# FFN of a two-layer encoder trunk: two tiles kept on chip as one down chunk in 8 PSUM banks, the last wo weights loaded ahead of the FFN's first, DRAM operands split in program order, operands at 512-byte starts

## The chip, the cores and the metric

The kernel runs on one core of a Trainium2 chip. The metric is device time in microseconds (us) of one launch on that core, as the median of several runs. One further run was profiled, and its trace is what the rows below come from. The engines are TensorE (PE; its weight loads are PEld), VectorE (DVE), ScalarE (ACT), GpSimd (POOL) and SyncE (SP), which issues most of the DMAs. PE's clock has two levels, 1.2 and 2.4 GHz; the profile gives the granted clock of a stretch as a share of the higher one.

## What is computed

An encoder of two layers over 1024 tokens of width 1024: a mixer with a residual, then a gated feed-forward network (FFN) with a residual, then a final norm. The change touches the FFN, the end of each mixer and the addresses of the operands.

```python
def reference(x, ...):
    h = x
    for layer in range(2):
        hn = rmsnorm(h, attn_norm_g[layer])
        if layer % 2 == 0:
            mix = hybrid_pool_mla(hn, ...)   # pooling and latent attention, then @ w_out
        else:
            mix = diff_block(hn, ...)        # differential attention, then @ w_out
        h = h + mix
        h = h + swiglu(rmsnorm(h, ffn_norm_g[layer]), ffn_w_gate[layer], ffn_w_up[layer], ffn_w_down[layer])
    return rmsnorm(h, final_norm_g)

def swiglu(h, w_gate, w_up, w_down):          # hidden width 2816 = 22 tiles of 128
    return (jax.nn.silu(h @ w_gate) * (h @ w_up)) @ w_down
```

## The kernel before

Everything is held transposed: 8 row tiles `o` of 128 features by 1024 tokens, the tokens in two halves `hf` of 512. Each fp32 product is made of three matmuls on operands split into a high and a low part (`mm3`, L160 to L164): high by high (L162), high by low (L163), low by high (L164). ACT makes the high part by a cast, DVE (in places POOL) the low part by a subtraction, so each weight tile needs a DMA into a raw tile, a cast and a subtraction before PE can use it. The raw tiles of the `weights` pool have 3 slots, the split ones 4 (`whi`, `wlo`).

**End of a mixer (`residual`, L674 on).** The mixer's output projection runs over the row tiles in the order of `PAIRS` (0, 4, 1, 5, 2, 6, 3, 7). DVE adds each result to the residual (L683; the tiles are `hT` in layer 0, `hB` in layer 1), and ACT and DVE make the FFN's operands from it: `b11`, `t2` and others, high and low parts of sums and differences of quarters of the activations. The weights of the projection are `wob0` to `wob7` in layer 0 (named `raw_wob`, `whi_wob`, `wlo_wob`) and `wdb0` to `wdb7` in layer 1. For the last pair, 3 and 7, half 0 of both is computed before half 1 of both; half 1 of a tile is written after DVE has added its half 0. In the loop the FFN's first weights (`load_first`: `raw_a11`, `raw_a21`, `raw_a22`, and their sums `s1` to `s3` on POOL, L776) are loaded at `i == 3`.

**Gate and up (`gate_up`).** For each of 22 tiles `ff` of the hidden width, 7 products (`PRODUCTS`, a Strassen scheme on the 2 by 2 quarters) of 4 mm3 each, so 84 matmuls, go into 4 banks. `prep` splits a weight tile for a product (L794, L795); every fifth pair lies in `s_pool` (names `wh`, `wl`), the others in the `weights` pool (`whi`, `wlo`). `after` turns the banks into an activation tile `u` of 128 by 1024; tiles 0 to 19 go to DRAM (`asp`), 20 and 21 stay.

**Down.** `CHUNKS` sets the order: (20), (21), then five chunks of 4 tiles. A step is one chunk and one row tile `o`: for each half, a bank takes 3 matmuls for each tile of the chunk, and DVE adds the bank to `hd` (L948), which `down_begin` has fetched from DRAM on POOL's queue. There are 8 banks. A step's weights (`raw_d`, L928; `whi_d`, `wlo_d`) are 128 columns wide for each tile. From chunk (21) on, the operands of the next chunks are fetched (`araw`), cast (`ah`, L916) and subtracted (`al`, L917) by `slot`.

What stands on an engine runs in the order of a list scheduler, which works on the program's order and its own estimates; `tc.keep_in_program_order` and `tc.high_priority` steer it.

Of the kernel before, what the change touches and what calls it, by code (L numbers as in the profile page):

```python
# [43 lines left out]
def encoder_trunk(ctx: ExitStack, tc: tile.TileContext, A: dict):  # L44
# [9 lines left out]

    def pad(p, name):

        p.tile([P, 8], F32, name=name, tag="pad", bufs=1)

    pad(spool, "pad_s")
    pad(rpool, "pad_r")  # L60

# [50 lines left out]
    dve.memset(onec, 1.0)  # L112
    pad(cpool, "pad_c")
    ones_f = cpool.tile([P, P], F32, name="ones_f")
# [562 lines left out]
    def residual(norm, spill, load, run, ffn):  # L677
# [9 lines left out]
        for i, o in enumerate(PAIRS[:6]):  # L687
            for j in (i, i + 1, i + 2):
                load(PAIRS[j])
            ps = run(o, (0, 1))  # L690
            for hf in range(2):
                norm.square(o, hf, out(o, hf, ps[hf]))
            if i % 2:
                norm.firsts(i // 2, hT)
                if i > 2:
                    norm.rest(i // 2 - 1, hT, (1,))
            elif i:
                norm.rest(i // 2 - 1, hT, (0,))
            if i == 3:
                ffn.load_first()  # L700
# [38 lines left out]
    class FeedForward:  # L739
# [67 lines left out]
        def after(self, ff, i):  # L807
# [34 lines left out]
        def gate_up(self, ps):  # L842
# [38 lines left out]
            for k, (ff, i) in enumerate(work):  # L881
# [9 lines left out]
                if k == len(work) - 2:  # L891
                    self.next_weights(0)
                    self.next_weights(1)
                self.product(ff, i)
                if k < len(work) - 1:
                    self.after(ff, i)
                if (ff, i) == (NFF - 2, 6):
                    self.keep_halves(ff)

        def keep_halves(self, ff):  # L900
            u = self.keep[ff]["u"]
            hi, lo = ([self.g_pool.tile([P, HT], F32R, tag="raw", name=f"a{w}{i}_{self.L}_{ff}", bufs=6)
                       for i in range(2)] for w in "hl")
            for i in range(2):
                act.copy(hi[i], u[:, half(i)])
                dve.tensor_tensor(lo[i], u[:, half(i)], f(hi[i]), ALU.subtract)
            self.seen[ff] = [(hi[i], lo[i]) for i in range(2)]


        seen = property(lambda self: self.__dict__.setdefault("_seen", {}))  # L910

        def slot(self, ff, src):
# [3 lines left out]
            act.copy(hi, src)  # L916
            dve.tensor_tensor(lo, src, f(hi), ALU.subtract)  # L917
            self.seen[ff] = [(hi[:, half(i)], lo[:, half(i)]) for i in range(2)]

        def operand(self, ff):  # L920
            raw = self.a_pool.tile([P, T], F32, tag="araw", name=f"araw{self.L}_{ff}", bufs=2)
            nc.sync.dma_start(raw, asp[ff])
            self.slot(ff, raw)

# [26 lines left out]
        def down_begin(self, a_pool, hpool, n_slots):  # L951
# [6 lines left out]
            self.after(NFF - 1, 6)  # L958
            self.slot(NFF - 1, self.keep[NFF - 1]["u"])
            self.held = 1  # L960
            self.ahead = [ff for c in self.CHUNKS[2:] for ff in c]
            self.down_steps(range(8), None, None)

        def down_steps(self, ks, finish, between_halves):
            last = len(self.CHUNKS) - 1
            for k in ks:
                c, o = self.steps[k]
                self.next_weights(k + 2)

# [7 lines left out]
                if o == 7 and c:  # L977
                    self.held -= len(self.CHUNKS[c])
# [624 lines left out]
```

## Time and profile before

| | us |
|---|---|
| median of 3 runs | 2656.02 (2654.16 to 2659.57) |
| profiled run | 2657.84 |
| span of its trace | 2656.1 |
| PE busy | 2538.1 (96%) |
| DVE busy | 1705.3 (64%) |
| ACT busy | 1065.4 (40%) |

PE is busy in all but 118 us of the span, so what matters is where those lie and how long a matmul takes. A row of the timeline shows when an instruction started, how long it took, and in brackets how long its engine had stood before it and what released it. A matmul's own duration overlaps the next; the step from one start to the next is its price.

### The profile page before, as it was taken

Reading aid. Unit: us, or ns where it says so; the run is one execution under the profiler, and the core shown is the slowest. Engines: PE = TensorE matmul, PEld = TensorE weight load, DVE = VectorE, ACT = ScalarE, POOL = GpSimd, SP = SyncE. Lnnn points to the kernel's source line nnn. Section 1 sums busy time; section 2 is a strip of 40 time slices with the busy share of each in tenths; the row PEclk is TensorE's granted clock in tenths of the full one; section 3 lists DMA queues with packets and bytes.
Section 4 is the critical chain, followed back from the end, with each engine's and each line's share of the span. In section 5 each row is a group of like instructions: output and inputs, shape, how many; then the busy total and the mean of one; then the engine's idle time right before and its main releaser. Section 6 shows DMA issues by size and latency. Waiting matters only on the chain. (4 is left out here: it accounts for less than half of the span.)

```text
span 2656.1 us, 31575 instructions
## 1 busy us (share of the span) xinstructions
PE 2538.1 (96%) x11334; PEld 1993.0 (75%) x11334; DVE 1705.3 (64%) x2932; ACT 1065.4 (40%) x1888; POOL 759.5 (29%) x582
## 2 busy tenths in 40 slices
PE   8999999899999989999999999999989999989997
PEld 6777887688888868886666666666768888877886
DVE  7467776866666664455677677676586566656444
ACT  4236666533333321243555555544353333332222
POOL 4224443422222100033434343333342222210002
PEclk9999999999999999999999999999999999999998
DMA  3010001622222152322111111114452222233321
GB/s 132 32 44 15 17 9 42 171 79 92 75 92 72 56 179 80 111 99 63 33 40 44 36 48 33 36 44 159 131 134 86 81 78 89 76 122 113 111 76 64
DMA packets 129580, 205.50 MB, mean 77 GB/s; under 512 B 11664, under 2 KB 56720, under 8 KB 129424
## 3 DMA queue, kind: packets, MB, share of 16 engines
q1 hardware_dynamic: 123088, 187.76, 21.3%
q0 software_dynamic: 6336, 15.73, 2.4%
q8 instruction: 89, 1.46, 0.2%
q14 instruction: 67, 0.55, 0.1%
HBM read 145.25 MB, written 46.66 MB: 72 GB/s over the span
## 5 line engine op out<-in xcount | busy, mean ns | idle before, releaser
L162 PE MATMUL d<-ah,whi_d 128*128 128x512 f32 x640 | 254.4, 398 | 22.5 <-DVE hd L948 17.0
L948 DVE TENSOR_TENSOR hd<-hd,d 128x512 f32<-128x512 f32 x224 | 150.4, 684 | 184.8 <-PE d L164 184.7
L163 PE MATMUL d<-al,whi_d 128*128 128x512 f32 x640 | 254.3, 397 | 0.0
L164 PE MATMUL d<-ah,wlo_d 128*128 128x512 f32 x640 | 248.1, 393 | 0.4 <-DVE wlo_d L933 0.3
L509 ACT CAST pth<-pt 128x512 fp32r<-128x512 f32 x256 | 145.6, 586 | 159.4 <-PE pt L506 156.2
L776 POOL TENSOR_TENSOR s<-s,raw_a 128x512 f32<-128x512 f32 x88 | 117.0, 1330 | 319.5 <-DVE wlo_s L795 231.0
L510 DVE TENSOR_TENSOR ptl<-pt,pth 128x512 fp32r<-128x512 f32 x256 | 169.9, 686 | 54.6 <-ACT pth L509 53.0
L1226 DVE CUSTOM_DVE_ANT_0 e<-s,nd 128x512 f32<-128x512 f32 x256 | 169.1, 686 | 42.6 <-PE s L1224 39.7
L776 POOL TENSOR_TENSOR s<-raw_a,raw_a 128x512 f32<-128x512 f32 x88 | 117.7, 1337 | 262.4 <-DVE wlo_s L795 207.0
L794 ACT CAST whi_s<-s 128x512 fp32r<-128x512 f32 x142 | 88.1, 621 | 242.9 <-PE p L163 232.8
L1239 ACT ACTIVATE e<-e,nm 128x1024 f32<-128x1024 f32 x128 | 146.4, 1147 | 68.5 <-DVE nm L1234 68.4
L506 PE MATMUL pt<-ident,e 128*128 128x128 f32 x1024 | 156.6, 281 | 9.1 <-POOL e L500 4.6
L162 PEld LDWEIGHTS d<-ah,whi_d 128*128 128x128 f32 x640 | 121.5, 190 | 56.0 <-issue 17.2
L506 PEld LDWEIGHTS pt<-ident,e 128*128 128x128 f32 x1024 | 125.5, 144 | 48.2 <-DVE ptl L510 11.2
L932 ACT CAST whi_d<-raw_d 128x512 fp32r<-128x512 f32 (+1 forms) x104 | 53.9, 521 | 260.4 <-PE d L163 208.7
L164 PEld LDWEIGHTS d<-ah,wlo_d 128*128 128x128 f32 x640 | 121.3, 190 | 27.9 <-DVE wlo_d L933 1.9
L163 PEld LDWEIGHTS d<-al,whi_d 128*128 128x128 f32 x640 | 121.7, 190 | 25.5 <-DVE al L917 0.8
L1248 POOL TENSOR_SCALAR e<-e,c 128x1024 f32<-128x1024 f32 x48 | 57.3, 1193 | 276.7 <-DVE c L1244 99.9
L794 ACT CAST whi_a<-raw_a 128x512 fp32r<-128x512 f32 x106 | 65.7, 621 | 138.2 <-PE p L163 137.6
L1221 PE MATMUL s<-KS,QS 128*128 128x512 f32 x256 | 97.2, 428 | 24.4 <-DVE mx L1226 23.3
L1249 POOL TENSOR_TENSOR e<-e,e 128x1024 f32<-128x1024 f32 x48 | 117.1, 2439 | 3.4
L795 DVE TENSOR_TENSOR wlo_s<-s,whi_s 128x512 fp32r<-128x512 f32 x142 | 115.4, 813 | 0.1
(492 smaller groups left out, 6861.6 us busy)
## 6 DMA issues: line engine op xcount, KB each, us to landing
raw_a<-in_w_gate_dram SPq DMA_DIRECT2D x88, 256.0 KB, 2.9
raw_a<-in_w_up_dram SPq DMA_DIRECT2D x88, 256.0 KB, 2.6
asp<-u SPq DMA_DIRECT2D x40, 512.0 KB, 2.9
araw<-asp SPq DMA_DIRECT2D x40, 512.0 KB, 3.7
raw_d<-in_w_down_dram SPq DMA_DIRECT2D x80, 256.0 KB, 2.8
hd<-hs POOLq DMA_DIRECT2D x16, 512.0 KB, 8.5
acc_f<-sq_f POOLq DMA_DIRECT2D x28, 256.0 KB, 4.3
hT<-in_xT_dram SPq DMA_DIRECT2D x16, 256.0 KB, 5.4
```

The lines of the kernel that those rows point to most:

```text
L162: pe.matmul(ps, sh, mh, start=start, stop=False, skip_group_check=onto)
L163: pe.matmul(ps, sh, ml, start=False, stop=False, skip_group_check=onto)
L164: pe.matmul(ps, sl, mh, start=False, stop=stop, skip_group_check=onto)
L506: pe.transpose(pt[:, blk(j)], es[j][:, blk(kt)], ident)
L509: act.copy(hi, pt)
L510: dve.tensor_tensor(lo, pt, f(hi), ALU.subtract)
L776: pool.tensor_tensor(t, r[ff, a], r[ff, b], op)
L794: act.copy(hi, self.raws[ff, n])
L948: dve.tensor_tensor(s, s, b, ALU.add)
L1226: dve.tensor_tensor_reduce(out=e[m][:, half(hf)], in0=ps[m], in1=nd[:, k0 + hf * HT : k0 + hf * HT + HT], scale=1.0, scalar=-3.0e38, op0=A ...
L1239: act.activation(e[m], e[m], AF.Exp, bias=nm, scale=slope, accum_out=l)
L1249: pool.tensor_tensor(e0, e0, e1, ALU.add)
```

## The change

Five parts. The pads that shift the pools are resized (`pad_s` is dropped, `pad_r` is 480 bytes, `pad_c` is 64, and `gsub` moves to the constants), which puts the start of the `weights` pool at byte 18432 of a partition instead of 18368, that is at 0 instead of 448 within 512, and with it the tiles of `temps`, `gate_up` and several other pools. Of some 9,940 matmuls with 512 columns, 7,440 had a stationary operand that started 448 bytes into a 512-byte line, and 2,044 such a moving operand; now none has. In `residual` the weights of the projection are loaded one step earlier and the FFN's first ones one step later. Chunks (20) and (21) become one, (20, 21), whose weights come as 4 loads of 512 columns (`first_weights`) and whose 16 results are evicted once instead of twice. Tile 21's half 0 is finished and split one product earlier. Preps of tile 1, and the splits of the DRAM operands, are held in program order.

```diff
-    pad(spool, "pad_s")
-    pad(rpool, "pad_r")
+    pad(rpool, "pad_r", 480)
...
-    pad(cpool, "pad_c")
+    pad(cpool, "pad_c", 64)
...
-            for j in (i, i + 1, i + 2):
+            for j in range(i, min(i + 4, 8)):
                 load(PAIRS[j])
...
-            if i == 3:
+            if i == 4:
                 ffn.load_first()
...
-        CHUNKS = ((20,), (21,), (0, 1, 2, 3), (4, 5, 6, 7), (8, 9, 10, 11), (12, 13, 14, 15), (16, 17, 18, 19))
+        CHUNKS = ((20, 21), (0, 1, 2, 3), (4, 5, 6, 7), (8, 9, 10, 11), (12, 13, 14, 15), (16, 17, 18, 19))
...
+            pin = tc.keep_in_program_order if ff == 1 else lambda x: x
...
-            act.copy(hi, self.raws[ff, n])
-            dve.tensor_tensor(lo, self.raws[ff, n], f(hi), ALU.subtract)
+            pin(act.copy(hi, self.raws[ff, n]))
+            pin(dve.tensor_tensor(lo, self.raws[ff, n], f(hi), ALU.subtract))
...
                 if i == 0:
-                    self.after(ff, i)
+                    with tc.high_priority(offset=150):
+                        self.after(ff, i)
...
+                if (ff, i) == (NFF - 1, 5):
+                    self.finish_half(ff, 0)
+                    self.keep_half(ff, 0, "c", 4)
...
+        def keep_half(self, ff, hf, tag, bufs):
+            u = self.keep[ff]["u"][:, half(hf)]
+            hi, lo = (self.g_pool.tile([P, HT], F32R, tag=tag, name=f"a{w}{hf}_{self.L}_{ff}", bufs=bufs)
+                      for w in "hl")
+            act.copy(hi, u)
+            dve.tensor_tensor(lo, u, f(hi), ALU.subtract)
+            self.seen.setdefault(ff, {})[hf] = hi, lo
...
+        def first_weights(self, q):
+
+            L, ffs = self.L, self.CHUNKS[0]
+            raw = wpool.tile([P, HT], F32, tag="raw", name=f"raw_d{L}_f{q}", bufs=3)
+            nc.sync.dma_start(
+                raw.rearrange("p (a b) -> p a b", a=2),
+                A["w_down"][L][ffs[0] : ffs[-1] + 1, :, 2 * q * P : (2 * q + 2) * P].rearrange("a p b -> p a b"))
...
-            self.slot(NFF - 1, self.keep[NFF - 1]["u"])
-            self.held = 1
-            self.ahead = [ff for c in self.CHUNKS[2:] for ff in c]
-            self.down_steps(range(8), None, None)
+            self.keep_half(NFF - 1, 1, "c", 4)
+            self.held = 0
+            self.ahead = [ff for c in self.CHUNKS[1:] for ff in c]
+            for g in range(2):
+                os = range(4 * g, 4 * g + 4)
+                if g:
+                    self.next_operands()
+                    self.first_weights(2)
+                    self.first_weights(3)
+                banks = {}
+                for j, ff in enumerate(self.CHUNKS[0]):
+                    for hf in range(2):
+                        for o in os:
+                            if j == 0:
+                                banks[o, hf] = self.bank(f"d{L}_f_{o}_{hf}")
+                            mm3(banks[o, hf], *self.ws["first", o // 2].block(2 * j + o % 2), *self.seen[ff][hf],
+                                j == 0, j == 1)
+                            if j:
+                                s = self.h[o][:, half(hf)]
+                                dve.tensor_tensor(s, s, banks[o, hf], ALU.add)
```

On DVE in layer 1, from the finish of the last activation tile `u1_21` to the second row tile's additions, there stood before:

```order
L838 TENSOR_TENSOR u1_21_20424<-u1_21_20424,rb_f1_17159 128x1024
L917 TENSOR_TENSOR al1_0_20714<-araw1_0_20711,ah1_0_20713 128x1024
L917 TENSOR_TENSOR al1_1_20720<-araw1_1_20717,ah1_1_20719 128x1024
L917 TENSOR_TENSOR al1_21_20569<-u1_21_20424,ah1_21_20568 128x1024
L933 TENSOR_TENSOR wlo_d1_0_6_20637<-raw_d1_0_6_20638,whi_d1_0_6_20636 128x128
L948 TENSOR_TENSOR hd1_0_20547<-hd1_0_20547,d1_0_0_0_20578 128x512
L948 TENSOR_TENSOR hd1_0_20547<-hd1_0_20547,d1_0_0_1_20583 128x512
```

The same place now, where `d1_f_0_0` is the bank of row tile 0, half 0, of the joint chunk:

```order
L919 TENSOR_TENSOR u1_21_20325<-u1_21_20325,rb_f1_17060 128x512
L913 TENSOR_TENSOR al1_1_21_20476<-u1_21_20325,ah1_1_21_20475 128x512
L1000 TENSOR_TENSOR hd1_0_20454<-hd1_0_20454,d1_f_0_0_20479 128x512
L1000 TENSOR_TENSOR hd1_0_20454<-hd1_0_20454,d1_f_0_1_20495 128x512
L1000 TENSOR_TENSOR hd1_1_20455<-hd1_1_20455,d1_f_1_0_20483 128x512
L1000 TENSOR_TENSOR hd1_1_20455<-hd1_1_20455,d1_f_1_1_20499 128x512
L955 TENSOR_TENSOR wlo_d1_1_0_20668<-raw_d1_1_0_20669,whi_d1_1_0_20667 128x512
L1000 TENSOR_TENSOR hd1_2_20456<-hd1_2_20456,d1_f_2_0_20487 128x512
```

The splits of the DRAM operands (`al1_0`, `al1_1`) stood ahead of the first addition and stand behind the eighth now, outside this piece.

On SP near the end of layer 0's mixer, the difference in the order of the loads (`hs0` is the residual's copy to DRAM):

```order
+L134 DMA raw_wob3_0_0_4672<-in_wo_b_dram 128x512
 L684 DMA hs0_4499<-hT0_93 128x512 x2
-L768 DMA raw_a21_0_0_4721<-in_w_up_dram 128x512
+L134 DMA raw_wob7_0_0_4727<-in_wo_b_dram 128x512
 L684 DMA hs0_4499<-hT4_97 128x512 x2
+L768 DMA raw_a11_0_0_4774<-in_w_gate_dram 128x512
 L684 DMA hs0_4499<-hT1_94 128x512 x2
-L768 DMA raw_a22_0_0_4723<-in_w_up_dram 128x512
+L768 DMA raw_a21_0_0_4776<-in_w_up_dram 128x512
 L684 DMA hs0_4499<-hT5_98 128x512 x2
-L134 DMA raw_wob3_0_0_4733<-in_wo_b_dram 128x512
```

The last two weights of the projection moved ahead of the three first weights of the FFN; in layer 1 `raw_wdb3` and `raw_wdb7` moved in the same way.

On ACT in layer 1's residual, the cast of `whi_wdb3` stood here before, behind the scaling of the second pair:

```order
L649 ACTIVATE sq_f1_1_0_16874<-hB1_15705 128x512
L640 ACTIVATE b11h1_f1_16725<-hB1_15705,cols_88 128x512
L649 ACTIVATE sq_f1_1_1_16879<-hB1_15705 128x512
L664 ACTIVATE x_f1_0_16882<-hB0_15704,cols_88 128x512
L135 CAST whi_wdb3_0_16957<-raw_wdb3_0_0_16959 128x512
L637 CAST t1h0_f1_16743<-t1_f1_0_16883 128x512
L637 CAST t2h0_f1_16731<-t2_f1_0_16884 128x512
L637 CAST t3h0_f1_16737<-x_f1_0_16882 128x512
L135 CAST whi_wdb7_0_17006<-raw_wdb7_0_0_17008 128x512
```

And now:

```order
L135 CAST whi_wdb3_0_16797<-raw_wdb3_0_0_16799 128x512
L649 ACTIVATE sq_f1_1_0_16781<-hB1_15606 128x512
L640 ACTIVATE b11h1_f1_16626<-hB1_15606,cols_87 128x512
L649 ACTIVATE sq_f1_1_1_16786<-hB1_15606 128x512
L664 ACTIVATE x_f1_0_16789<-hB0_15605,cols_87 128x512
L637 CAST t1h0_f1_16644<-t1_f1_0_16790 128x512
L637 CAST t2h0_f1_16632<-t2_f1_0_16791 128x512
L135 CAST whi_wdb7_0_16852<-raw_wdb7_0_0_16854 128x512
```

The cast of `whi_wdb3` moved ahead by four places and that of `whi_wdb7` by one, and the loads of both stand ahead of the FFN's on SP, as in layer 0.

## Rows read from the trace of the kernel before

**Rows 1.** The page, part 1: busy us, share of the span, instructions.
```profile
PE 2538.1 (96%) x11334; PEld 1993.0 (75%) x11334; DVE 1705.3 (64%) x2932; ACT 1065.4 (40%) x1888; POOL 759.5 (29%) x582
```
**Rows 2.** Stretches: us; busy us (xinstructions) of each engine; clock, DMA share, GB/s.
```profile
515.00:540.00 25.00, 20.52 (x88) 16.03 (x88) 17.33 (x30) 10.29 (x18) 12.41 (x11) 0.86 0.36 82
...
937.90:974.50 36.60, 27.08 (x98) 19.08 (x96) 29.95 (x51) 10.93 (x21) 0.00 (x0) 0.86 0.57 197
974.50:1195.00 220.50, 220.50 (x962) 180.42 (x963) 110.46 (x155) 60.06 (x88) 21.09 (x16) 1.00 0.32 102
...
2376.80:2416.70 39.90, 26.50 (x98) 19.63 (x96) 33.89 (x56) 14.05 (x25) 1.92 (x4) 0.87 0.67 241
```
**Rows 3.** Waits of PE: line waited for, total us, times, longest us.
```profile
PE d L162 <- DVE hd L948: 17.0, 6, 7.6
PE od L162 <- DVE hB L683: 7.6, 1, 7.6
...
PE d L162 <- ACT whi_d L932: 5.5, 4, 1.9
PE ob L162 <- DVE hT L683: 4.8, 1, 4.8
...
PE p L162 <- DVE u L824: 3.9, 2, 3.3
```
**Rows 4.** Timeline of PE, start of down in layer 1: start, us, instruction, wait.
```profile
2382.05 0.39 PE L164 MATMUL d<-ah,wlo_d 128*128 128x512 f32 x1
2390.02 0.77 PE L162 MATMUL d<-ah,whi_d 128*128 128x512 f32 x1 [7.58 <-DVE hd L948]
2390.59 0.63 PE L163 MATMUL d<-al,whi_d 128*128 128x512 f32 x1
```
**Rows 5.** Timeline of DVE, the same place.
```profile
2387.86 1.22 DVE L917 TENSOR_TENSOR al<-u,ah 128x1024 fp32r<-128x1024 f32 x1
...
2389.20 1.28 DVE L948 TENSOR_TENSOR hd<-hd,d 128x512 f32<-128x512 f32 x2
```
**Rows 6.** Groups by line and form on DVE, layer 1's down: busy us, mean ns.
```profile
L948 DVE TENSOR_TENSOR hd<-hd,d 128x512 f32<-128x512 f32 x112 | 75.0, 683 | 93.4 <-PE d L164 93.3
L917 DVE TENSOR_TENSOR al<-araw,ah 128x1024 fp32r<-128x1024 f32 x20 | 24.4, 1222 | 12.1 <-ACT ah L916 11.9
```
**Rows 7.** DMA issues between 2370 and 2420: count, KB each, us to landing.
```profile
hd<-hs POOLq DMA_DIRECT2D x8, 512.0 KB, 9.1
```
**Rows 8.** Timeline of PE, three products of tile 21, layer 1, first matmuls.
```profile
2360.37 0.39 PE L162 MATMUL p<-t2h_f,whi_s 128*128 128x512 f32 x1
...
2363.12 0.39 PE L162 MATMUL p<-t3h_f,wh_s 128*128 128x512 f32 x1
...
2365.84 0.39 PE L162 MATMUL p<-t1h_f,whi_s 128*128 128x512 f32 x1
```
**Rows 9.** Timeline of PE, layer 1's last chunk, 48 matmuls apart.
```profile
2592.56 0.39 PE L162 MATMUL d<-ah,lwh 128*128 128x512 f32 x1
...
2603.44 0.39 PE L162 MATMUL d<-ah,lwh 128*128 128x512 f32 x1
```
**Rows 10.** Timeline of PE, layer 1's residual, the last pair of row tiles.
```profile
1940.78 0.80 PE L162 MATMUL od<-yh,whi_wdb 128*128 128x512 f32 x1 [7.59 <-DVE hB L683]
```
**Rows 11.** Timeline of ACT, layer 1's residual.
```profile
1918.62 0.62 ACT L135 CAST whi_wdb<-raw_wdb 128x512 fp32r<-128x512 f32 x1 [4.55 <-DMA raw_wdb<-in_w_do_dram]
...
1924.58 0.62 ACT L135 CAST whi_wdb<-raw_wdb 128x512 fp32r<-128x512 f32 x1 [3.78 <-DMA raw_wdb<-in_w_do_dram]
```
**Rows 12.** Timeline of DVE, the same residual.
```profile
1919.80 1.37 DVE L638 TENSOR_TENSOR t1l_f<-t_f,t1h_f 128x512 fp32r<-128x512 f32 x1 [2.23 <-ACT t1h_f L637]
...
1926.38 0.75 DVE L641 SCALAR_TENSOR_TENSOR b21l_f<-hB,cols,b21h_f 128x512 fp32r<-128x512 f32 x1 [2.15 <-ACT b21h_f L640]
```
**Rows 13.** Timeline of DVE, layer 0: in the residual, and at the start of gate and up.
```profile
485.45 0.69 DVE L136 TENSOR_TENSOR wlo_wob<-raw_wob,whi_wob 128x512 fp32r<-128x512 f32 x1 [1.91 <-ACT whi_wob L135]
...
524.70 0.69 DVE L795 TENSOR_TENSOR wl_s<-s,wh_s 128x512 fp32r<-128x512 f32 x1 [3.08 <-ACT wh_s L794]
```

More of the change, by code (lines that the diff above doesn't have):

```diff
@@ L53, in encoder_trunk, with pad @@
     rpool = tc.alloc_tile_pool(name="edge", bufs=1, side="right")
-    def pad(p, name):
-        p.tile([P, 8], F32, name=name, tag="pad", bufs=1)
-    pad(spool, "pad_s")
-    pad(rpool, "pad_r")
+    def pad(p, name, n):
+        p.tile([P, n // 4], F32, name=name, tag="pad", bufs=1)
+    pad(rpool, "pad_r", 480)
     def new_pool(name, side, bufs=1):
@@ L121, in encoder_trunk @@
     nc.sync.dma_start(cols, A["cols"])
+    gsub = cpool.tile([P, 1], F32, name="gsub")
     def col(i):
@@ L897, in gate_up, with finish_half, operand @@
                 if (ff, i) == (NFF - 2, 6):
[L898 to L907, printed above, removed]
+                    for hf in range(2):
+                        self.keep_half(ff, hf, "raw", 6)
+                if (ff, i) == (NFF - 1, 5):
[8 more added lines that the diff above has]
+            self.seen.setdefault(ff, {})[hf] = hi, lo
+        def finish_half(self, ff, hf):
+            g, u = (self.keep[ff][k][:, half(hf)] for k in "gu")
+            dve.tensor_tensor(u, u, g, ALU.mult)
+            dve.tensor_tensor(u, u, self.norm.rb[:, half(hf)], ALU.mult)
         seen = property(lambda self: self.__dict__.setdefault("_seen", {}))
-        def slot(self, ff, src):
+        def operand(self, ff):
+            raw = self.a_pool.tile([P, T], F32, tag="araw", name=f"araw{self.L}_{ff}", bufs=2)
+            nc.sync.dma_start(raw, asp[ff])
             hi = self.a_pool.tile([P, T], F32R, tag=f"s{self.n_seen % self.n_slots}h", name=f"ah{self.L}_{ff}")
@@ L915, in slot @@
             self.n_seen += 1
-            act.copy(hi, src)
-            dve.tensor_tensor(lo, src, f(hi), ALU.subtract)
+            tc.keep_in_program_order(act.copy(hi, raw))
+            tc.keep_in_program_order(dve.tensor_tensor(lo, raw, f(hi), ALU.subtract))
             self.seen[ff] = [(hi[:, half(i)], lo[:, half(i)]) for i in range(2)]
[L920 to L923, printed above, removed]
+        def first_weights(self, q):
[4 more added lines that the diff above has]
+                A["w_down"][L][ffs[0] : ffs[-1] + 1, :, 2 * q * P : (2 * q + 2) * P].rearrange("a p b -> p a b"))
+            hi, lo = w_pair(f"d{L}_f{q}")
+            act.copy(hi, raw)
+            dve.tensor_tensor(lo, raw, f(hi), ALU.subtract)
+            self.ws["first", q] = W([(hi, lo)])
         def weights(self, c, o, pair):
@@ L958, in down_begin, with next_operands @@
             self.after(NFF - 1, 6)
-            self.slot(NFF - 1, self.keep[NFF - 1]["u"])
-            self.held = 1
-            self.ahead = [ff for c in self.CHUNKS[2:] for ff in c]
-            self.down_steps(range(8), None, None)
+            self.keep_half(NFF - 1, 1, "c", 4)
[9 more added lines that the diff above has]
+                for j, ff in enumerate(self.CHUNKS[0]):
+                    for hf in range(2):
+                        for o in os:
[6 more added lines that the diff above has]
+                                dve.tensor_tensor(s, s, banks[o, hf], ALU.add)
+            self.next_weights(8)
+            self.next_weights(9)
+        def next_operands(self):
+            while self.ahead and self.held < self.n_slots:
+                self.operand(self.ahead.pop(0))
+                self.held += 1
         def down_steps(self, ks, finish, between_halves):
@@ L968, in down_steps @@
                 self.next_weights(k + 2)
-                while c and self.ahead and self.held < self.n_slots:
-                    self.operand(self.ahead.pop(0))
-                    self.held += 1
+                self.next_operands()
                 for hf in range(2):
@@ L976, in down_steps @@
                         finish(o, hf, s)
-                if o == 7 and c:
+                if o == 7:
                     self.held -= len(self.CHUNKS[c])
```

7 lines of the change are left out of this document (4 added, 3 removed).

## The prediction

> **What bounds it now.** I read the page's busy times first: PE is busy for 2538 of 2656 us [rows 1], so time can be gained only where PE stands, where its clock is low, or on the price of a matmul. Then the table of stretches. In both FFNs gate and up, and the five large down chunks, have no gap: 220.5 us for 962 matmuls, a busy time equal to the stretch, clock 1.00 [rows 2], which is 229.2 ns a matmul. The gaps touched by this change lie where stages meet. The first two down chunks, 96 matmuls in each layer, take 36.6 us in layer 0 and 39.9 in layer 1, PE busy for 27.1 and 26.5, at clocks of 0.86 and 0.87 [rows 2]. The waits name who holds PE there: DVE's additions to `hd`, 17.0 us, and the casts of down weights, 5.5; and elsewhere the last pair of row tiles in the two residuals, 7.6 and 4.8, and the start of gate and up, 3.9 [rows 3].
>
> At 229.2 ns, 96 matmuls are 22.0 us. So these stretches hold 14.6 and 17.9 us too much, 32.5 together. Of layer 1's 17.9, 13.4 are gaps (39.9 less 26.5) and 4.5 are matmuls stretched by the clock (26.5 less 22.0): behind the wait of 7.58 us a matmul lasts 0.63 instead of 0.39 [rows 4], the lower of the two levels.
>
> **The joint chunk.** Why does PE wait 7.58 us? Of the old chunk (20), each bank takes three matmuls, 0.69 us, so the 8 banks are full after 5.5 us, and the first must have been added to `hd`. The last matmul before the wait starts at 2382.05; the addition starts at 2389.20 [rows 4, 5]. It was ready long before, but stood in DVE's queue behind the finish of tile 21 and three splits of 1.22 us, two of DRAM operands whose data was still being fetched, and one of tile 21.
>
> In the changed order the additions stand ahead of the DRAM splits, and three things move the due times. Eight banks now take 6 matmuls each, so PE needs the first bank back after 11.0 us instead of 5.5. Counting from the start of down, DVE has until then some seven operations of a half each (the finish, the two splits, a weight split), at about 0.69 us, and one silu on ACT between: the first addition falls at about 6.3, 4 us early. Tile 20's 24 matmuls cover 5.5 us in which tile 21's half 1 can be finished; half 0, finished a product earlier, is due at 5.5 and there at about 2.5; half 1 is due at 8.2 and there at about 6.3. The loads of `hd` take 9.1 us [rows 7] and are issued at the same point; they now have the same 4 us of slack.
>
> DVE's work for the 22 us is: 16 additions at 0.683, 10.9 us; four DRAM splits at 1.222, 4.9 [rows 6]; three weight splits and six half operations at about the price of an addition, 6.1. That is 21.9 in 22.0, where before it was busy for 33.9 in layer 1 [rows 2], with 16 more additions. This has no margin, but not all is due at the end: the last additions free banks that PE wants up to 5 us later. What is queued in a new place is the weight split `wlo_d1_1_0`, which in layer 1 stands between the fourth and the fifth addition: it waits for a cast on ACT that stands behind two casts of DRAM operands, and with it wait the additions that free the last banks of the second group, due at 12.3 to 13.0. I get 12.7 for that split. Three new loads of 256 KB stand ahead of the DRAM operands too. So I leave 1 us of waiting in layer 0 and 3 in layer 1. Bounds: all 32.5 is gained, or half of it. I take 28.5.
>
> **The addresses.** Does it cost anything to start a stationary operand 448 bytes into a line? The trace has both cases side by side. A product of 12 matmuls with `whi_s` (448) runs from 2360.37 to 2363.12, 2.75 us; the next, with `wh_s` from `s_pool` (0), to 2365.84, 2.72 [rows 8]. That is 2.5 ns a matmul, give or take 0.8 for the rounding. In down the tiles of layer 1's last chunk lie at 0: 48 matmuls take 10.88 us, 226.7 ns [rows 9], against 229.2 [rows 2], again 2.5. Of the 3,696 matmuls of gate and up four fifths have their weights in the `weights` pool, 2,957; of down's 2,112 all but 192. 4,877 times 2.5 ns is 12.2 us, the upper bound; nothing is the lower, since these tiles differ from the others by pool as well as by address. The agreement of two places makes me take 9.
>
> The Trainium skill speaks against this term: "TensorE: Matmul & The Clock Gate", Back-to-back issue gap, gives the step as the columns over the clock plus a constant, worked out some 216 ns for 512 columns, with no place for an address, and by it the term would be 0. No row here runs at that step: they show 226.7 and 229.2.
>
> **The residuals.** In layer 1 ACT waits 4.55 and 3.78 us for the raw tiles of `wdb3` and `wdb7` [rows 11], because the FFN's three raw tiles were loaded first into the same 3 slots, and DVE idles 2.23 and 2.15 behind ACT [rows 12]. From there on DVE works almost without a gap up to the addition that PE waits 7.59 us for [rows 10]. With those loads ahead, DVE is 4.4 us earlier and the wait falls to about 3.2; it may also be too short for the clock to fall, which by layer 1's down (two falls for 4.5 us) is worth about 2.2. DVE, whose order is otherwise the same, gives some back later. Bounds 0 and 9.8; I take 5. In layer 0 DVE idles only 1.91 for the same reason [rows 13], and its queue ahead of the addition, for which PE waits 4.8, is shorter by one operation; PE comes earlier by the waits for the casts that vanish, but meets the same DVE. Bounds -2 (the FFN's first weights now land later, with three sums on POOL behind them) and 4.8; I take 2.
>
> **The start of gate and up.** In layer 0 DVE stands 3.08 us before a weight split for tile 1 [rows 13], and PE then 3.3 for DVE [rows 3]; the stretch has 4.5 us of gaps and a clock of 0.86, worth 2.9 of its 20.5 [rows 2]. Held in program order, that split no longer stands there, but two more operations for the norm do. Bounds -2 and 7.4; I take 2.5. Layer 1's smaller gaps I cost at nothing. The pins on the DRAM splits are part of the first term.
>
> **Sum.** 28.5 + 9 + 5 + 2 + 2.5 = 47. The profiled run took 2657.84, 1.8 over the median, its span 1.7 less than that; 2657.84 less 47 is 2610.8, and on the scale of the median 2609.
>
> **Rivals.**
> *The addresses give nothing.* For it: the two pools differ in who writes them and when, and a 0.03 us difference is three units of a row's last digit. Against it: down shows it over 48 matmuls. 2609 + 9 = 2618.
> *DVE becomes the bound of the joint chunk.* For it: 21.9 us of work in 22.0, and in order. A wait moves from the first additions to the last ones, or to chunk 1's first operands, and a wait of several us would lower the clock again. Against it: DVE has 11 us less to do than before. With half of the excess kept, 16.2 gained instead of 28.5: 2621.
> *The residuals and the start of gate and up give nothing*, because DVE's work there, not the order of loads, sets the pace: 9.5 less, 2618.
> *Slower: aligned operands collide.* If now both operands start at 0 of a line, for nearly all of some 9,940 matmuls, and fetching the two at once costs time, each may be dearer. It decides from (47 - 9) over 9,940, 3.8 ns a matmul, that is from a step of 233. At 5 ns, twice the difference seen the other way, it costs 50 and gives 2656 - 38 + 50 = 2668. Against it: in [rows 8] the product with aligned weights is the cheaper one.
>
> **How the numbers follow.** The forecast has a chance of 0.52, the rivals 0.21, 0.13, 0.11 and 0.03. 2609 is the forecast's. For the range I go up to the first two rivals together, 2630, with 2 for the run's own spread, and down by the upper bounds of the addresses, 3, both boundaries, 4, and half of what the other three could still give, 6: 2596 to 2632. The bounds all at once, 2589, are left outside. A change within 0.2%, 5.3 us, is about what a measurement cannot tell from none. Faster has 0.95, since three of the rivals lie 35 us or more below the time before; within 0.2% has 0.02, slower 0.03.
>
> **What would show it.** The first addition of layer 1's down starts about 6 us after down does, PE has no wait over 3 us among the joint chunk's 96 matmuls, and they take 22 to 25 us at a clock near 1.0. A product with `whi` takes 2.72 us, as one with `wh` does, and the five large chunks some 218 us. ACT does not wait for `raw_wdb`, and PE's wait for `hB` is about 3 us. It would be wrong if the step stayed at 229, if waits for `hd`, `wlo_d` or `al` of some 8 us stood at the end of the joint chunk, or if PE waited at the FFN's first product for POOL's sums.

## The result, and the profile after

| | before | changed |
|---|---|---|
| median of 5 runs, us | 2656.02 (2651.89 to 2659.57) | 2614.55 (2614.14 to 2619.80) |
| profiled run, us | 2657.84 | 2614.45 |
| span, us | 2656.1 | 2612.7 |
| mean granted clock | 0.978 | 0.983 |

The ratio of the times is 0.9849, with a 95% interval of 0.9835 to 0.9864. The change took 41.5 us off the median; 47 were predicted.

Part 1 of the page of the changed kernel answers to [rows 1]:

```profile
PE 2517.5 (96%) x11334; PEld 1989.8 (76%) x11334; DVE 1688.7 (65%) x2882; ACT 1060.5 (41%) x1866; POOL 757.8 (29%) x582
```

PE has the same 11334 matmuls and is busy for 20.6 us less: they became cheaper, by their step or by the clock. The other 22.8 us of the span were gaps. The stretches of the changed kernel that answer to [rows 2], with its own bounds (the start of gate and up, layer 0's joint chunk, its five large chunks, layer 1's joint chunk; columns as there):

```profile
515.00:540.00 25.00, 21.04 (x88) 16.23 (x87) 18.90 (x30) 10.29 (x18) 11.56 (x11) 0.93 0.43 110
937.00:959.20 22.20, 22.11 (x98) 17.97 (x97) 15.65 (x23) 6.58 (x9) 0.00 (x0) 1.00 0.76 277
959.20:1178.00 218.80, 218.71 (x963) 180.17 (x962) 112.36 (x157) 61.31 (x89) 20.89 (x16) 1.00 0.32 104
2350.18:2374.30 24.12, 22.12 (x98) 17.98 (x97) 16.81 (x26) 7.07 (x10) 1.80 (x4) 1.00 0.75 272
```

The joint chunks take 22.2 and 24.1 us instead of 36.6 and 39.9, without a fall of the clock, and the large chunks 218.8 for 963 matmuls, 227.2 ns each. The waits of PE, against [rows 3]:

```profile
PE s L1263 <- DVE mx L1268: 23.2, 20, 1.7
PE ob L162 <- DVE hT L683: 9.5, 1, 9.5
...
PE od L162 <- DVE hB L683: 5.1, 1, 5.1
...
PE d_f L162 <- DVE hd L1000: 2.0, 1, 2.0
...
PE p L162 <- DVE u L825: 1.6, 1, 1.6
```

The 17.0 us for `hd` became 2.0 and the waits for the casts of down weights are gone. But the residuals still wait, and in layer 0 longer: 9.5 instead of 4.8. (The first row is the mixer of layer 1, which the change leaves alone: 23.3 us before.)

To see where the rest went I cut each trace at the first matmul of each stage. The numbers are us more or less than before; the eight touched stages are the two residuals (R), the two gate and up parts (G), the joint chunks (J) and the large chunks (D) of layers 0 and 1; "rest" is the untouched time. The lower rows are the runs of the next section.

| | R0 | G0 | J0 | D0 | R1 | G1 | J1 | D1 | touched | rest | span |
|---|---|---|---|---|---|---|---|---|---|---|---|
| changed | 0.7 | -2.2 | -14.4 | -1.7 | -3.3 | -1.2 | -15.7 | -1.2 | -39.2 | -4.2 | 2612.7 |
| changed_again | 0.4 | -2.2 | -14.3 | -1.0 | -3.1 | -2.4 | -14.4 | -1.4 | -38.4 | -0.4 | 2617.3 |
| pads_alone | -0.1 | -3.4 | -0.2 | -1.9 | -0.6 | -3.2 | -0.1 | -1.7 | -11.2 | -5.2 | 2639.7 |
| pads_undone | 1.3 | 0.8 | -14.3 | 0.6 | -3.4 | 1.9 | -13.3 | -0.1 | -26.6 | -7.5 | 2622.0 |
| joint_alone | 0.8 | 0.2 | -14.3 | 0.4 | -0.3 | 0.1 | -13.7 | -0.1 | -26.9 | -7.8 | 2621.4 |
| order_undone | 0.5 | -5.1 | -14.8 | -1.5 | 0.0 | -1.8 | -12.8 | -1.8 | -37.3 | -0.2 | 2618.6 |
| pins_undone | -0.3 | 0.0 | -14.4 | -1.6 | -3.3 | 1.0 | -16.7 | -1.2 | -36.5 | -9.5 | 2610.1 |
| sums_early | 1.6 | -2.4 | -14.8 | -1.0 | -2.4 | -1.3 | -13.5 | -1.8 | -35.6 | -4.2 | 2616.3 |
| last_pair_first | -5.3 | 0.9 | -14.6 | -1.3 | -6.5 | 2.1 | -12.9 | -1.8 | -39.5 | -5.6 | 2611.0 |
| chunk1_pinned | 0.4 | -2.2 | -14.8 | 3.4 | -3.3 | -1.3 | -18.1 | -0.9 | -36.8 | -6.1 | 2613.2 |
| both | -5.3 | 2.4 | -14.8 | -1.0 | -6.4 | 2.2 | -18.1 | -0.9 | -41.9 | -3.0 | 2611.2 |
| both_pool | -1.4 | 0.5 | -14.4 | -1.1 | -6.5 | 3.5 | -18.1 | -0.9 | -38.3 | -6.9 | 2611.0 |
| start_256 | 0.6 | -2.2 | -14.8 | -1.5 | -3.4 | -1.3 | -13.9 | -1.8 | -38.4 | -5.8 | 2611.9 |

The untouched part alone differs by 9 us between traces, and is shorter than in the one trace of before in every row, with old pads and with new. So edits worth less than that are read in their own stage and not from the span, and each from one trace of its kernel (two of the changed one).

### The profile page after: what moved, and what is told of

Its sections match the earlier page's. It is cut to its first block, busy times and chain, and to the rows that moved or that the text cites. A ratio compares the mean times of both kernels' runs of the same rounds, so it can differ in the third digit from the quotient of the medians.

```text
span 2612.7 us, 31389 instructions
## 1 busy us (share of the span) xinstructions
PE 2517.5 (96%) x11334; PEld 1989.8 (76%) x11334; DVE 1688.7 (65%) x2882; ACT 1060.5 (41%) x1866; POOL 757.8 (29%) x582
## 5 line engine op out<-in xcount | busy, mean ns | idle before, releaser
L163 PE MATMUL d<-al,whi_d 128*128 128x512 f32 x576 | 224.8, 390 | 0.4 <-DVE al L932 0.3
L164 PE MATMUL d<-ah,wlo_d 128*128 128x512 f32 x576 | 224.2, 389 | 0.0
L162 PE MATMUL d<-ah,whi_d 128*128 128x512 f32 x576 | 224.2, 389 | 0.0
L970 DVE TENSOR_TENSOR hd<-hd,d 128x512 f32<-128x512 f32 x160 | 109.6, 686 | 169.1 <-PE d L164 168.6
L1268 DVE CUSTOM_DVE_ANT_0 e<-s,nd 128x512 f32<-128x512 f32 x256 | 169.2, 686 | 42.3 <-PE s L1266 39.5
L506 PEld LDWEIGHTS pt<-ident,e 128*128 128x128 f32 x1024 | 124.6, 144 | 48.0 <-DVE ptl L510 11.2
L163 PEld LDWEIGHTS d<-al,whi_d 128*128 128x128 f32 x576 | 108.1, 188 | 24.5 <-DVE al L932 2.2
L162 PEld LDWEIGHTS d<-ah,whi_d 128*128 128x128 f32 x576 | 108.1, 188 | 22.3
L164 PEld LDWEIGHTS d<-ah,wlo_d 128*128 128x128 f32 x576 | 108.1, 188 | 22.3
L954 ACT CAST whi_d<-raw_d 128x512 fp32r<-128x512 f32 x72 | 44.4, 621 | 195.4 <-PE d L163 187.3
L1263 PE MATMUL s<-KS,QS 128*128 128x512 f32 x256 | 96.0, 423 | 24.1 <-DVE mx L1268 23.2
```

The lines of the kernel that those rows point to most:

```text
L162: pe.matmul(ps, sh, mh, start=start, stop=False, skip_group_check=onto)
L163: pe.matmul(ps, sh, ml, start=False, stop=False, skip_group_check=onto)
L164: pe.matmul(ps, sl, mh, start=False, stop=stop, skip_group_check=onto)
L506: pe.transpose(pt[:, blk(j)], es[j][:, blk(kt)], ident)
L1268: dve.tensor_tensor_reduce(out=e[m][:, half(hf)], in0=ps[m], in1=nd[:, k0 + hf * HT : k0 + hf * HT + HT], scale=1.0, scalar=-3.0e38, op0=A ...
```

## The experiments

The diffs are against the changed kernel unless they say otherwise. Each median stands beside that of the kernel before on the same chip: 2656.18 for the first four, 2656.03 for the next four, 2653.26 for the last.

**pads_undone**: the old pads, all else as changed.

```diff
-    pad(rpool, "pad_r", 480)
+    pad(spool, "pad_s")
+    pad(rpool, "pad_r")
...
-    pad(cpool, "pad_c", 64)
+    pad(cpool, "pad_c")
```

> The changed kernel with the old pads, so that the weights pool starts at 448 of a 512-byte line again; all else as changed. Theory A, the start of the stationary operand costs time: matmuls with whi go back from 226.8 to about 229 ns, and 4,877 of them in gate and up and down cost 11 us, 2626; if the layer-1 mixer's 5 us, which nothing in the prediction explains, were the addresses too, 2630. Rival, the step depends on the pool or on what runs beside it: the step stays at 227 and the time at 2615.

2626.24 us (2623.77 to 2627.68), ratio 0.9887 (0.9872 to 0.9902). G and D of both layers lose 3.1, 3.2, 2.2 and 1.2 us against the changed kernel, 9.7 together. The step of the matmuls shows it. First matmuls (L162) of products in this run:

```profile
2341.91 0.39 PE L162 MATMUL p<-t3h_f,wh_s 128*128 128x512 f32 x1
...
2344.63 0.39 PE L162 MATMUL p<-t1h_f,whi_s 128*128 128x512 f32 x1
...
2347.38 0.39 PE L162 MATMUL p<-b21h_f,whi_a 128*128 128x512 f32 x1
```

and in the changed kernel, against [rows 8]:

```profile
2320.20 0.39 PE L162 MATMUL p<-t1h_f,whi_s 128*128 128x512 f32 x1
...
2322.92 0.39 PE L162 MATMUL p<-b21h_f,wh_a 128*128 128x512 f32 x1
...
2325.64 0.39 PE L162 MATMUL p<-t4h_f,whi_a 128*128 128x512 f32 x1
```

With the old pads a product with `wh` takes 2.72 us and the next, with `whi`, 2.75; with the new ones both take 2.72.

**pads_alone**: the kernel before with the new pads and nothing else (the lines above in reverse).

> The kernel before with the new pads and nothing else. Theory A: 2656 less 11 is 2645, or 2640 if the layer-1 mixer's 5 us come from the addresses; both residuals and the start of gate and up as long as before to within 2 us. Rival: no change, 2656.

2638.49 us (2635.99 to 2641.44), ratio 0.9935 (0.992 to 0.9949). G and D gain 3.4, 3.2, 1.9 and 1.7, 10.2 together; no other touched stage moves by more than 0.6. The median falls by more, 17.7. The expectation's other value, 2640 if layer 1's mixer gained by the addresses too, is nearer to it, but that mixer is 4.5 us shorter than before in this trace and 5.4 shorter in that of joint_alone, which has the old pads. So the runs tie only the 10 us in G and D to the addresses.

**joint_alone**: the changed kernel with the old pads, the old order of loads and without the pins of tile 1.

```diff
-            for j in range(i, min(i + 4, 8)):
+            for j in (i, i + 1, i + 2):
...
-            if i == 4:
+            if i == 3:
...
-            pin = tc.keep_in_program_order if ff == 1 else lambda x: x
+            pin = lambda x: x
...
-                    with tc.high_priority(offset=150):
-                        self.after(ff, i)
+                    self.after(ff, i)
```

> The changed kernel without the pads, the order of loads, the pins of tile 1's preps and the priority: what is left is the joint chunk of tiles 20 and 21 with its early half and the DRAM operands held in order. Theory: the two joint chunks take about 22.3 and 24.3 us at 229 ns a matmul in place of 36.6 and 39.9, 30 us less, 2626. Rival, the gain at the boundary came in part from the weights that the other parts moved: half, 2641.

2623.28 us (2621.60 to 2631.66), ratio 0.9885 (0.9864 to 0.9907). J0 and J1 gain 14.3 and 13.7, and all other touched stages together lose 1.1. With pads_alone's 11.2 this makes 38.1 of the 39.2 that the whole change has in these stages: order and pins are left with 1.1. The medians do not add up so: joint_alone is 32.9 below before and pads_alone 17.7, together 50.6 where the whole change gives 41.5. What is too much there lies in the untouched part and is not explained.

**order_undone**: the first two hunks of joint_alone's diff alone.

> The changed kernel with the old order of loads in the residuals (three steps of weights ahead, the FFN's first weights at the fourth step). Theory, the order of loads moves a wait but gains little, since DVE sets the pace and POOL's sums now fall on it: layer 0's residual 0 to 1 us shorter, layer 1's 2 to 3 longer, 2616 to 2618. Rival, as predicted, the order of loads is worth 7 us: 2621.5.

2616.46 us (2614.34 to 2620.36), ratio 0.9853 (0.9838 to 0.9868), as the changed kernel. R1 loses the 3.3 us that the order had gained, and PE waits there as before ([rows 10]); but G0 and G1 gain 2.9 and 0.6, so that over these four stages the old order is 0.3 shorter. Timeline of PE in this run, the start of gate and up in layer 0, then the last pair of layer 1:

```profile
525.89 0.48 PE L162 MATMUL p<-t4h_f,whi_a 128*128 128x512 f32 x1 [0.16 <-DVE vh_f L194]
...
1920.27 0.79 PE L162 MATMUL od<-yh,whi_wdb 128*128 128x512 f32 x1 [7.85 <-DVE hB L683]
```

**pins_undone**: the last two hunks alone.

> The changed kernel without the pins on tile 1's preps and without the priority of the first after. Theory, they gain in layer 0, where a split of tile 1 no longer stands ahead of the norm, and lose in layer 1, where nothing stood there: gate and up 1.5 us longer in layer 0 and 1 shorter in layer 1, together 2615. Rival, as predicted, they are worth 2.5 us: 2617.

2611.97 us (2610.34 to 2626.78), ratio 0.985 (0.9815 to 0.9886): no difference to be seen in the time. In the trace G0 and G1 each lose 2.2 us, and this wait of PE in layer 0 shows why: without the pins DVE splits a weight of tile 1 ahead of the norm's `v_f`. In layer 1 a gain had been expected, and the loss came there too. Over R and G of both layers the pins are worth 3.5 with the new order of loads; with the old order they are worth nothing (order_undone is within 0.1 of joint_alone and pads_alone added).

```profile
528.03 0.76 PE L162 MATMUL p<-t4h_f,whi_a 128*128 128x512 f32 x1 [6.27 <-DVE vl_f L195]
```

**sums_early**: the FFN's first weights one step earlier again, the new order of the projection's weights kept.

```diff
-            if i == 4:
+            if i == 3:
```

> The changed kernel with the FFN's first weights loaded at the fourth step again, but the weights of the projection still four ahead, so that wob3 comes before them and wob7 behind. Theory, POOL's three sums leave the place in which DVE's queue decides, where two DVE operations took 1.8 and 2.8 us instead of 0.75 beside them: the wait of 9.5 us falls by about 3, and the sums are in time for the FFN's first products: 2610 to 2612. Rival, the late sums cost nothing: 2614.5, or more, if ACT waits for wob7 again.

2614.65 us (2611.42 to 2618.07), ratio 0.9844 (0.9825 to 0.9863). Nothing is gained: R0 is 1.0 longer than in the changed kernel and R1 0.9. POOL's sums now stretch DVE earlier, at 474 instead of 488, and PE waits twice. The rival's reason came as well: ACT waits for the last weights of the projection again, 4.11 us for a `raw_wob` (DVE stands 1.47 behind that cast) and 2.23 for a `raw_wdb`. The timeline of DVE in this run, then that of PE:

```profile
474.35 1.77 DVE L641 SCALAR_TENSOR_TENSOR b21l_f<-hT,cols,b21h_f 128x512 fp32r<-128x512 f32 x1
```

```profile
484.26 0.47 PE L162 MATMUL ob<-bh,whi_wob 128*128 128x512 f32 x1 [3.31 <-DVE hT L683]
493.65 0.80 PE L162 MATMUL ob<-bh,whi_wob 128*128 128x512 f32 x1 [5.17 <-DVE hT L683]
```

**last_pair_first**: the additions of the last pair ahead in DVE's queue.

```diff
-                out(o, hf, ps[n][hf])
+                with tc.high_priority(offset=150):
+                    out(o, hf, ps[n][hf])
```

> The changed kernel with the additions of the last pair of row tiles at a higher priority, so that on DVE they stand some eight (layer 0) and six (layer 1) operations further ahead. Theory A, PE waits for those additions because of what stands ahead of them: the waits of 9.5 and 5.1 us fall by 5 and 4, and with them a stretch at the lower clock goes, 2604 to 2608. Theory B, DVE's whole load sets the pace: the operations passed over are due at once in the FFN's first products, the waits move there and the time stays within 3 us of 2614.5.

2612.84 us (2605.79 to 2614.09), ratio 0.9832 (0.9811 to 0.9852), not to be told from the changed kernel. The waits fall to 4.20 and 2.51, and R0 and R1 gain 6.0 and 3.1 over the changed kernel. G0 and G1 give 3.1 and 3.3 back. PE's timeline in this run, the two last pairs, then layer 1's start of gate and up:

```profile
493.88 0.80 PE L162 MATMUL ob<-bh,whi_wob 128*128 128x512 f32 x1 [4.20 <-DVE hT L683]
...
1909.84 0.50 PE L162 MATMUL od<-yh,whi_wdb 128*128 128x512 f32 x1 [2.51 <-DVE hB L683]
1926.69 0.50 PE L162 MATMUL p<-t2h_f,whi_s 128*128 128x512 f32 x1 [0.65 <-ACT t2h_f L637]
1927.91 0.50 PE L163 MATMUL p<-t2l_f,whi_s 128*128 128x512 f32 x1 [0.72 <-DVE t2l_f L638]
```

The first 40 us of gate and up in layer 1 now hold waits for `u`, `dh_f`, `wlo_s` and `t2` of 4.7 us, where the changed kernel has 1.9: the same work of DVE, met later. In layer 0 this is true in part. The waits of PE in the whole of G0 rise by 1.4 us only, and the rest of the 3.1 goes with the granted clock: in the first 40 us of G0 it is 0.91 here and 0.96 in the changed kernel, while in R0 it rose from 0.92 to 0.97.

**chunk1_pinned**: the first weight split of the second chunk held in program order in both layers.

```diff
+            pin = tc.keep_in_program_order if (c, o) == (1, 0) else lambda x: x
-            act.copy(hi[:, : n * P], raw[:, : n * P])
-            dve.tensor_tensor(lo[:, : n * P], raw[:, : n * P], f(hi[:, : n * P]), ALU.subtract)
+            pin(act.copy(hi[:, : n * P], raw[:, : n * P]))
+            pin(dve.tensor_tensor(lo[:, : n * P], raw[:, : n * P], f(hi[:, : n * P]), ALU.subtract))
```

> The changed kernel with the weight split of chunk 1's first step held in program order, behind all additions of the joint chunk. Theory, that split, which waits for ACT, is what PE's 2.0 us wait in layer 1 hangs on: the wait goes, and the joint chunk of layer 1 takes 22 us instead of 24, 2612.5. Rival, the split is then late for chunk 1, whose first matmul waits as long: 2614.5.

2616.53 us (2614.08 to 2618.34), ratio 0.985 (0.9833 to 0.9868). J1 gains 2.3 us, so the 2.0 us wait there was this split's. Layer 0 loses 5.0 in D0, since there a split now comes too late for the second chunk: 3.3 us of waiting, as this row of PE's timeline shows, and a granted clock of 0.92 around it (958 to 980), where the changed kernel has 1.00:

```profile
965.02 0.79 PE L164 MATMUL d<-ah,wlo_d 128*128 128x512 f32 x1 [3.33 <-DVE wlo_d L956]
```

**both**: last_pair_first, and the pin of chunk1_pinned in layer 1 alone (`(L, c, o) == (1, 1, 0)`). **both_pool**: the same with the low parts of `wob` made on POOL (a third argument `pool` to `load_w` in layer 0). **changed_again**: the changed kernel on the same chip.

> The changed kernel with the additions of the last pair first (as in last_pair_first) and the pin on chunk 1's first weights in layer 1 alone. If stages add up: 2.7 less from the first and 2.0 less from the second, 4.7 below the changed kernel run beside it. If DVE's load sets the pace there as well, the second is given back and it is 2 to 3 below.

> As both, with the low parts of layer 0's projection weights made on POOL instead of DVE, which takes four subtractions of 0.69 us off DVE in the residual. If DVE's load is what PE waits for in layer 0: residual and start of gate and up 2 to 3 us shorter than in both. If DVE loses to POOL, which holds it up while it reads, what it gains: no change, or up to 3 longer.

> The changed kernel itself, beside the two before on the same chip: 2614.5 again, to within 2; in another profiled execution the stretch of layer 0 before the FFN and the layer-1 mixer, which the change does not touch, differ by up to 6 us from the first, as they did among the runs so far.

2611.91 (2610.38 to 2612.92), 2616.05 (2612.75 to 2617.00) and 2613.88 us (2609.55 to 2619.13); ratios 0.9845 (0.983 to 0.9861), 0.9863 (0.9844 to 0.9881) and 0.9854 (0.9834 to 0.9875). `both` is 2.0 below the changed kernel, with intervals that overlap: not shown to be faster, though its touched stages are 2.7 and 3.5 below those of the two traces of the changed kernel. With POOL's help the median is 4.1 higher, again with intervals that overlap, and R0 is 3.9 longer than in `both`: PE waits 7.99 us where `both` waits 1.63 and 2.25. Not all of that is POOL holding DVE up, since DVE also stands 2.51 us there behind ACT's cast of a weight of the FFN (`wh_a`). PE's timeline in both_pool, the last pair of layer 0:

```profile
492.49 0.80 PE L162 MATMUL ob<-bh,whi_wob 128*128 128x512 f32 x1 [7.99 <-DVE hT L683]
```

**start_256**: pads that put nearly all operands at 256 within 512 instead of 0.

```diff
-    pad(rpool, "pad_r", 480)
+    pad(rpool, "pad_r", 224)
...
-    pad(cpool, "pad_c", 64)
+    pad(cpool, "pad_c", 320)
```

> The changed kernel with pad_c 256 bytes larger and pad_r 256 smaller, so that nearly all stationary and moving operands of 512-column matmuls start at 256 of a 512-byte line. Theory, what costs is that a block of 128 columns lies across two 512-byte lines: matmuls with whi take 229 ns as before the change, and those with wh, which lay at 0, now too. Rival, a start at a multiple of a smaller size is enough and only 448 was bad: 226.8 for all.

One run, 2613.64 us. The touched stages together are within 0.8 of the changed kernel's, and in PE's timeline a product with `whi` still takes 2.72:

```profile
2340.74 0.39 PE L162 MATMUL p<-b21h_f,whi_a 128*128 128x512 f32 x1
...
2343.46 0.39 PE L162 MATMUL p<-t4h_f,whi_a 128*128 128x512 f32 x1
...
2346.18 0.39 PE L162 MATMUL p<-b22h_f,whi_s 128*128 128x512 f32 x1
```

## Why the prediction was right, and where it was wrong

**The joint chunk: right.** 28.5 were predicted; J0 and J1 give 30.1 in the changed kernel, 28.7 in its second trace and 28.0 in joint_alone. The mechanism is the one described, down to the split that it named. What no run separates is the joint chunk itself, the early half of tile 21 and the order of the DRAM splits: the 28.0 belongs to the three together. Layer 1's timeline of PE, then DVE, then ACT:

```profile
2350.12 0.39 PE L162 MATMUL d_f<-ah,whi_d_f 128*128 128x512 f32 x1
...
2363.49 0.39 PE L164 MATMUL d_f<-ah,wlo_d_f 128*128 128x512 f32 x1
2365.87 0.50 PE L162 MATMUL d_f<-ah,whi_d_f 128*128 128x512 f32 x1 [2.00 <-DVE hd L1000]
```

```profile
2356.44 0.69 DVE L1000 TENSOR_TENSOR hd<-hd,d_f 128x512 f32<-128x512 f32 x1
...
2364.53 0.69 DVE L955 TENSOR_TENSOR wlo_d<-raw_d,whi_d 128x512 fp32r<-128x512 f32 x1 [3.49 <-ACT whi_d L954]
2365.14 2.47 DVE L1000 TENSOR_TENSOR hd<-hd,d_f 128x512 f32<-128x512 f32 x4
```

```profile
2360.43 1.05 ACT L931 CAST ah<-araw 128x1024 fp32r<-128x1024 f32 x1 [4.84 <-DMA araw<-asp]
2362.93 1.05 ACT L931 CAST ah<-araw 128x1024 fp32r<-128x1024 f32 x1 [1.45 <-DMA araw<-asp]
2363.88 1.13 ACT L954 CAST whi_d<-raw_d 128x512 fp32r<-128x512 f32 x2
```

Down starts at 2350.12 and the first addition at 2356.44, 6.3 us later, as worked out. `wlo_d1_1_0` stands at 14.4 after the start (12.7 estimated), behind a cast on ACT that stands behind two casts of DRAM operands, which wait for their data, and the four additions after it free a bank 2.0 us late, inside the 3 left for it. The rival in which DVE becomes the bound did not come: DVE is busy for 16.8 us of layer 1's 24.1, not the 21.9 counted, because some of the splits and the last additions fall behind the stretch.

**The addresses: right in size, and in part in the reason.** 9 were predicted; alone they give 10.2 in G and D, and undoing them costs 9.7. But a stationary operand that starts at 448 is not dear by itself, as the last section shows. The Trainium skill ("TensorE: Matmul & The Clock Gate", Back-to-back issue gap) gives a step without a term for an address, and the trace decides against it: 229.2 ns before, 227.2 now. The rival in which aligned operands collide is excluded by the same rows.

**The residuals and the start of gate and up: the step that failed in size.** 5 + 2 + 2.5 = 9.5 were predicted. R0 gives -0.7 and R1 3.3. G0 and G1 give 3.5, of which the addresses alone account for 6.6 (pads_alone), so that their starts lost 3.1. That makes -0.5 (0.7 in the second trace), and joint_alone and pads_alone leave 1.1 for the same edits. What failed is the order of loads, put at 5 + 2: what it gains in R1 it loses in G0 and G1 (order_undone). The pins, put at 2.5, are worth 3.5, but only against what the new order costs. The rival that gave all this nothing has the number right. Its reason, that DVE's work and not the order of loads sets the pace, is shown in part only.

On the median the time came out 5.5 above the forecast. The touched stages fell 7.8 short of 47: 10 are missing here, and the joint chunk and the addresses gave 2.2 more than forecast. The remaining 2.3 of the 41.5 came from the untouched part. No edit here explains them, so that much is luck.

Three sentences of the prediction show it. The first is "the wait falls to about 3.2" in layer 1. ACT no longer waits for the raw tiles of `wdb`, but the wait only passed to the next load. SP stands until POOL's sums are done with a raw tile: for 6.2 us before, ahead of a load of `raw_wdb`, and for 6.4 now, ahead of the FFN's fourth weight (`raw_a12`). The waits of SP, before and after:

```profile
SPq L134 <- POOL s L776: 6.2, 1, 6.2
```

```profile
SPq L768 <- POOL s L776: 6.4, 1, 6.4
```

So ACT waits 4.55 us as before, for another weight, and DVE stands behind it, with the split `wl_a` ahead of the additions in its queue. ACT and DVE in the changed kernel, against [rows 11, 12]:

```profile
1907.40 0.62 ACT L795 CAST wh_a<-raw_a 128x512 fp32r<-128x512 f32 x1 [4.55 <-DMA raw_a<-in_w_gate_dram]
```

```profile
1908.05 0.69 DVE L796 TENSOR_TENSOR wl_a<-raw_a,wh_a 128x512 fp32r<-128x512 f32 x1 [2.50 <-ACT wh_a L795]
```

DVE lost two idle times of 2.23 and 2.15 and got one of 2.50. The prediction counted the loads that moved ahead and not the one behind them. PE's wait fell from 7.59 to 5.13.

The second is "it may also be too short for the clock to fall": it fell, the matmul behind the wait takes 0.63. For layer 0, "PE comes earlier by the waits for the casts that vanish, but meets the same DVE" was right and I still priced it at a gain of 2. PE's last pair of layer 0 before, then the last pairs in the changed kernel, against [rows 10], and the start of gate and up between them:

```profile
498.33 0.80 PE L162 MATMUL ob<-bh,whi_wob 128*128 128x512 f32 x1 [4.82 <-DVE hT L683]
```

```profile
499.38 0.80 PE L162 MATMUL ob<-bh,whi_wob 128*128 128x512 f32 x1 [9.50 <-DVE hT L683]
499.97 0.63 PE L163 MATMUL ob<-bl,whi_wob 128*128 128x512 f32 x1
...
528.40 0.50 PE L201 MATMUL bc_f<-dh_f,ones_r 128*128 128x512 f32 x1 [0.97 <-DVE dh_f L199]
531.09 0.68 PE L162 MATMUL p<-t4h_f,whi_a 128*128 128x512 f32 x1 [1.58 <-DVE u L825]
...
1915.65 0.80 PE L162 MATMUL od<-yh,whi_wdb 128*128 128x512 f32 x1 [5.13 <-DVE hB L683]
1916.24 0.63 PE L163 MATMUL od<-yl,whi_wdb 128*128 128x512 f32 x1
```

Layer 0's PE starts its last pair at 499.38, 1.1 us later than before, for all the waits for casts that it lost (3.1 us); 0.6 of this is that the whole stage started later. From 483 to 499 DVE has no gap in its queue. In the 8 us ahead of that it stands for 4.0 us, for ACT and for a DMA of the norm (`acc_f`), so it is not short of time throughout. Two of its operations are stretched by POOL's sums, which stand at that place now. DVE, then POOL:

```profile
488.61 1.79 DVE L665 SCALAR_TENSOR_TENSOR t_f<-hT,cols,x_f 128x512 f32<-128x512 f32 x1
...
490.92 2.81 DVE L666 SCALAR_TENSOR_TENSOR t_f<-hT,cols,t_f 128x512 f32<-128x512 f32 x1
```

```profile
488.42 1.43 POOL L776 TENSOR_TENSOR s<-raw_a,raw_a 128x512 f32<-128x512 f32 x1 [0.99 <-DMA raw_a<-in_w_up_dram]
...
490.40 1.55 POOL L776 TENSOR_TENSOR s<-s,raw_a 128x512 f32<-128x512 f32 x1
491.63 1.54 POOL L776 TENSOR_TENSOR s<-raw_a,raw_a 128x512 f32<-128x512 f32 x1
```

Such an operation takes 0.75 us elsewhere, so the two cost DVE 3.1. The sums cost it about as much before the change, some 12 us earlier (3.3, on three operations), so they are no new cost:

```profile
476.99 1.89 DVE L641 SCALAR_TENSOR_TENSOR b21l_f<-hT,cols,b21h_f 128x512 fp32r<-128x512 f32 x1 [0.46 <-ACT b21h_f L640]
478.80 1.78 DVE L638 TENSOR_TENSOR t1l_f<-t_f,t1h_f 128x512 fp32r<-128x512 f32 x1
480.50 1.78 DVE L638 TENSOR_TENSOR t3l_f<-x_f,t3h_f 128x512 fp32r<-128x512 f32 x1
```

The Trainium skill ("SBUF — State Buffer", SBUF: two separate sides) has DVE operations with two inputs in SBUF and GpSimd's contend for a port pair that one holds for its whole instruction; the trace agrees: the sums of 1.43 to 1.55 us above stand beside the two operations of 1.79 and 2.81. But sums_early moved the sums away and gained nothing, since DVE is stretched earlier then and waits for a cast again. For the stretch without a gap the order on DVE counts: last_pair_first put the needed addition ahead, gained 9.1 us in R and lost 6.4 in G, to work put off and to the clock.

What stays open: `both` would need more runs to be told from the changed kernel, and no run takes `wl_a` from its place ahead of the additions, so what that wait is worth is not shown.

## What to carry to other kernels

A wait at a stage's border is worth its full length only if the engine waited for has slack behind it: the joint chunk took 16 additions off DVE and kept its gain, while a new order of DVE's queue gave two thirds of its gain back in the next stage. A load that is moved ahead pushes another back: ask what now stands last for the buffers. Cut the trace into stages and sum up an edit over the stage after it as well, since a run's untouched stages can differ by more than the edit. And compare the step of equal matmuls whose operands lie in different pools: 2 ns on some 5,000 matmuls was a quarter of this gain and showed in no wait.

## What the runs showed that was not expected

**A 512-byte start is not what makes a matmul cheap.** I set the starts of the operands, as the kernels are built, beside the mean steps in the trace (within 512 bytes; moving, stationary):

| kernel | products | starts | step, ns | matmuls |
|---|---|---|---|---|
| before | `p` (gate and up) | 0, 448 | 229.0 | 2891 |
| before | `p` (gate and up) | 0, 0 | 226.8 | 658 |
| before | `d` (down) | 0, 448 | 229.0 | 1784 |
| before | `od` (projection, layer 1) | 448, 448 | 227.3 | 149 |
| changed | `p` (gate and up) | 0, 0 | 226.75 | 3657 |

A step is counted here between two neighbours with the same starts. In start_256 nearly all lie at 256, 256, and the steps of `p` and `d` are 226.5 to 227. So a start of 448 is not dear by itself: what goes with some 2.2 ns here is a moving operand at 0 with a stationary one at 448. Not every such matmul pays: in the first row the steps behind the three matmuls of a product (L162, L163, L164) are 229.2, 231.5 and 226.1 ns, at the same starts. Whether the difference of the two starts decides, or something that goes with it, no run tells: it is argued from these pairs, not shown.

**An untouched stage can change by itself.** Layer 1's mixer holds 20 waits of up to 1.7 us for `mx` (23.3 us before, 23.2 after). The same stretch of 70 us has a granted clock of 0.95 in the trace of before (from 1614.37) and 1.00 in that of the changed kernel (from 1597.37). The changed kernel's own second trace shows that this needs no edit: over the 633 us of the mixer ahead of `ob` PE is busy for 604.0 us at a clock of 0.97, in the first trace for 597.9 at 0.98, with the same matmuls. The mixer alone differs by 8 us between the traces of this case, more than any edit to the residuals moved R and G together.
